# The first weight chunk of a two-layer decoder trunk: ScalarE's table by a copy of a constant, the first weights split ahead of the first features, the first token tile's three products ahead of the second tile's transposes

## The chip, the cores and the metric

One Trainium2 chip, one of its NeuronCores. The metric is the device time of one execution in microseconds (us); lower is better. The time before is a median of 3 executions.

## What is computed

A decoder trunk of two layers over 256 tokens of width 1024, all in float32. Each layer is a half-step SwiGLU feed-forward block, a mixer (a gated linear recurrence with 4 heads beside causal attention with forget gates and 8 heads), cross-attention to 256 memory tokens, and a second half-step feed-forward block. Every block has an RMS norm ahead of it and adds to the residual. The change lies in the first block alone, whose core is:

```python
def rms_norm(x, w):
    x32 = x.astype(jnp.float32)
    y = x32 * lax.rsqrt(jnp.mean(x32 * x32, axis=-1, keepdims=True) + EPS)
    return (y * w.astype(jnp.float32)).astype(x.dtype)

def swiglu(h, w_gate, w_up, w_down):
    return (jax.nn.silu(h @ w_gate) * (h @ w_up)) @ w_down

x = x + 0.5 * swiglu(rms_norm(x, ffn1_norm[l]), ffn1_w_gate[l], ffn1_w_up[l], ffn1_w_down[l])
```

## The kernel before, in words

**Products in three parts.** Each float32 matrix product is made of three products of rounded halves. An operand is split into a high part (rounded to the format that TensorE takes at full rate) and a low part (the operand minus its high part); high times high, high times low and low times high are summed in PSUM. So each piece of weights passes ScalarE, which writes `whi` from the raw piece (L149, or L153 where the norm's gain is multiplied in), and then VectorE, which writes `wlo` (L150 or L154). Features pass the same two engines in `put_split` (L368): ScalarE writes `xfh` (L369), VectorE `xfl` (L370).

**Weights.** `plan` lists all weight pieces in order of use; `fetch` starts their transfers on SyncE's queue into a pool of three `raw` buffers, 1 MB each. The first two pieces are fetched in four quarters of 128 x 512 each, and the input `x` (tile `xs`, in four blocks: token tile t, half j of the width) goes between them: block (0, 0), first quarter, block (1, 0), the other three quarters, blocks (0, 1) and (1, 1).

**The first chunk** (`first_chunk`, L482) makes the first 512 columns of `x @ w_gate` for both token tiles of 128, each into its own PSUM bank (`psa_[0]`, `psa_[1]`). The norm is not applied to the features here: its gain is multiplied into the weights and its scale applied afterwards, so the features are `x` itself, transposed. `turn(t, b)` transposes four 128 x 128 blocks of token tile t on TensorE into the PSUM tile `pt` (L495); `put` splits them; `split_block(i, k)` splits quarter k of weight piece i; `part(kt, t, which)` is one product of 128 x 128 features by 128 x 512 weights (L505), where `which` is 0 for high by high, 1 for high features by low weights (`wlo`), 2 for low features (`xfl`) by high weights. `block(kt)` is the six products of one quarter for both token tiles.

**What sets the order.** Inside `with in_order()` (L201) every engine's instructions are chained in the order in which the code is written, so that each engine takes them one by one as written and waits with all behind it when an operand is missing. The chunk is written as: transposes of the first token tile, six dummy transposes of the identity matrix into an unused bank (`warm_up`, L225), the split of these features, the split of the first weight quarter, two products of the first token tile, the transposes of the second token tile, their split, and then the rest. Ahead of it (L231 to L235) stand nine more dummy transposes and the transpose of the norm's gain (`g0t`, copied to `g0`, by which L153 and L154 multiply).

**ScalarE's table.** The building tools put an `ACT_TABLE_LOAD` ahead of the first ScalarE operation that needs one, here the split of the first features (L369).

Of the kernel before, what the change touches and what calls it, by code (L numbers as in the profile page):

```python
# [8 lines left out]
F32 = mybir.dt.float32  # L9
# [8 lines left out]
P = 128  # L18
# [27 lines left out]
def hymba_kernel(  # L46
# [6 lines left out]
    nc = tc.nc  # L53

    cp = ctx.enter_context(tc.tile_pool(name="cp", bufs=1))
# [10 lines left out]
    def nm(s):  # L66
        uid[0] += 1
        return f"{s}_{uid[0]}"

    def s4(shape, dt=F32, name="s4"):  # L70
        return sp.tile(shape, dt, name=nm(name), tag="s4")

    def small(cols, name="sc", rows=P, bufs=0):
        return sm.tile([rows, cols], F32, name=nm(name), tag=name, bufs=bufs or 4)

    def acc(name="acc"):
        return psa.tile([P, 512], F32, name=nm(name), tag="acc")

    def smp(name="smp"):
        return pss.tile([P, 512], F32, name=nm(name), tag="smp")  # L80
# [48 lines left out]
    def fetch(i):  # L129
        while len(raws) <= min(i, len(plan) - 1):  # L130
            src, nk, cw, _ = plan[len(raws)]
            r = rawp.tile([P, 4 * 520], F32, name=nm("raw"), tag="raw")
            rv = r[:, :nk * cw].rearrange("p (k c) -> p k c", k=nk)
            n = 4 if len(raws) < 2 else 1
            for k0 in range(0, nk, nk // n):
                nc.sync.dma_start(out=rv[:, k0:k0 + nk // n, :], in_=src[:, k0:k0 + nk // n, :])
                for t, j in ({0: [(1, 0)], 3: [(0, 1), (1, 1)]}.get(k0, []) if not raws else []):
                    load_x(t, j)
            raws.append(r)
# [5 lines left out]
    def split_k(i, sl, k, hi, lo):  # L145

        gk = plan[i][3]
        if gk is None:
            nc.scalar.copy(out=hi, in_=sl)  # L149
            nc.vector.tensor_tensor(out=lo, in0=sl, in1=hi.bitcast(F32), op=ALU.subtract)  # L150
        else:
            g = gcols[gk[0]][:, gk[1] + k:gk[1] + k + 1]
            nc.scalar.mul(hi, sl, g)  # L153
            nc.vector.scalar_tensor_tensor(out=lo, in0=sl, scalar=g, in1=hi.bitcast(F32), op0=ALU.mult,  # L154
                                           op1=ALU.subtract)

    def split_block(i, k):

        if k == 0:
            fetch(i + LA_D - 1)  # L160
            pieces.append([])
        cw = plan[i][2]
        if k % 2 == 0:
            slot[:] = [wp.tile([P, SLOT], F32R, name=nm(n), tag=n) for n in ("whi", "wlo")]
        sl = slice(k % 2 * cw, (k % 2 + 1) * cw)
        hi, lo = slot[0][:, sl], slot[1][:, sl]
        split_k(i, raws[i][:, k * cw:(k + 1) * cw], k, hi, lo)
        pieces[i].append((hi, lo))
        return [(hi, lo)]
# [30 lines left out]
    @contextmanager  # L200
    def in_order():  # L201

        traced = nc.cur_bb.bb.instructions
        n = len(traced)
        yield
        prev = {}
        for i in traced[n:]:
            if i.engine in prev:
                tc.add_manual_dep(i, prev[i.engine], mybir.DependencyInfo(mybir.DependencyClass.NoSync,
                                  mybir.DependencyReason.DATA), reason="in_order")  # L210
            prev[i.engine] = i.name
# [6 lines left out]
        fetch(i)  # L218


    ident = cp.tile([P, P], F32, name="ident")
    make_identity(nc, ident)
    warm = acc("warm")

    def warm_up(n):  # L225
        for i in range(n):
            nc.tensor.transpose(warm[:, (i % 4) * P:(i % 4 + 1) * P], ident, ident)
# [3 lines left out]
    with in_order():  # L231
# [1 line left out]
        nc.tensor.transpose(g0t[:, 0:8], grow, ident[0:8, 0:8])  # L233
        nc.vector.tensor_copy(out=g0, in_=g0t[:, 0:8])
        gcols["first"] = g0  # L235
    neghalf = cp.tile([P, 4], F32, name="neghalf")
    nc.vector.memset(neghalf, -0.5)

    lbr = cp.tile([24, P], F32, name="lbr")

# [100 lines left out]
    def inv_rms(ss, rs):  # L341
        ms = small(1, "ms")
        nc.vector.scalar_tensor_tensor(out=ms, in0=ss[:, 0:1], scalar=EPS, in1=ss[:, 1:2], op0=ALU.add, op1=ALU.add)
        nc.gpsimd.tensor_tensor(out=rs, in0=ms, in1=neghalf[:, 0:1], op=ALU.pow)  # L344

    def half(ap, j):
        return ap[:, j * 512:(j + 1) * 512]
# [20 lines left out]
    def put_split(hi, lo, src):  # L368
        nc.scalar.copy(out=hi, in_=src)  # L369
        nc.vector.tensor_tensor(out=lo, in0=src, in1=hi.bitcast(F32), op=ALU.subtract)  # L370
# [79 lines left out]
    def xstat(f, cw, ps):  # L450
        ps += [acc() for _ in range(NT)]
        for kb in range(2):
            pc = take()
            for j in range(4):
                c = 0.0
                for t in range(NT):
                    c += xmm(ps, f, 4 * kb + j, t, pc[j], cw)
                yield c
# [23 lines left out]
    def first_chunk(f, psa_, psb_):  # L482


        psa_ += [acc(), acc()]
        rs = [small(1, "rs0", bufs=2) for _ in range(NT)]
        sq = [s4([P, D], F32, "sq") for _ in range(NT)]
        sums = [small(2, "ss") for _ in range(NT)]
        pa = []

        def turn(t, b):
            pt = smp("pt")
            for j in range(4):
                kt = 4 * b + j
                nc.tensor.transpose(pt[:, j * P:(j + 1) * P], xs[:, t, kt * P:(kt + 1) * P], ident)  # L495
            return pt

        def put(pt, t, b):
            sl = slice(t * P, (t + 1) * P)
            put_split(f.h[b][:, :, sl], f.l[b][:, :, sl], pt.rearrange("p (k t) -> p k t", k=4))  # L500

        def part(kt, t, which):
            x = (f.hi, f.hi, f.lo)[which](kt, t)
            w = (pa[kt][0], pa[kt][1], pa[kt][0])[which]
            nc.tensor.matmul(psa_[t], lhsT=x, rhs=w, start=kt == 0 and which == 0, stop=kt == KT - 1 and which == 1)  # L505

        def block(kt, order=(0, 2, 1)):
            first = order[:2] if order[1] == 2 else order[:1]
            for t in range(NT):
                for w in first:  # L510
                    part(kt, t, w)
            for w in order[len(first):]:
                for t in range(NT):
                    part(kt, t, w)

        def squares(t):
            x = xs[:, t, :]
            nc.scalar.activation(sq[t][:, 0:512], half(x, 0), AF.Square, scale=1.0 / 32.0, accum_out=sums[t][:, 0:1])
            nc.vector.tensor_tensor_reduce(out=sq[t][:, 512:1024], in0=half(x, 1), in1=half(x, 1), scale=1.0 / 1024.0,
                                           scalar=0.0, op0=ALU.mult, op1=ALU.add, accum_out=sums[t][:, 1:2])  # L520

        with in_order():
            p0 = turn(0, 0)
            warm_up(6)
            put(p0, 0, 0)
            pa += split_block(0, 0)
            part(0, 0, 0)
            part(0, 0, 2)
            p1 = turn(1, 0)
            put(p1, 1, 0)  # L530
            part(0, 0, 1)
            for w in (0, 2, 1):
                part(0, 1, w)
            for kt in (1, 2):
                pa += split_block(0, kt)
                block(kt)
            pa += split_block(0, 3)
            p = [turn(t, 1) for t in range(NT)]
            block(3)
            pa += split_block(1, 0)  # L540
            for t in range(NT):
                put(p[t], t, 1)
            block(4, (0, 1, 2))
            for kt in (5, 6, 7):
                pa += split_block(1, kt - 4)
                if kt < 7:
                    squares(kt - 5)
                block(kt)
            taken[0] = 2
            for t in range(NT):  # L550
                inv_rms(sums[t], rs[t])
        yield 16 * T512
        yield from xstat(f, 512, psb_)
        rb = sq[0].rearrange("p (j t) -> p j t", j=8)
        pt = smp("rt")
        for t in range(NT):
            nc.vector.tensor_scalar(out=rb[:, t, :], in0=ident, scalar1=0.0, scalar2=rs[t], op0=ALU.mult, op1=ALU.add)
            nc.tensor.transpose(pt[:, t * P:(t + 1) * P], rb[:, t, :], ident)
        row = sm.tile([P, S], F32, name=nm("L"), tag="L", bufs=1)
        nc.vector.tensor_copy(out=row, in_=pt[:, 0:S])  # L560
        hrs = [small(1, "hrs0", bufs=2) for _ in range(NT)]
        for t in range(NT):
            nc.vector.tensor_scalar(out=hrs[t], in0=rs[t], scalar1=0.5, scalar2=None, op0=ALU.mult)
        return rs, hrs, row
# [652 lines left out]
```

## Time and profile before

| What | Value |
|---|---|
| median of 3 executions | 1234.5 us (1234.41 to 1234.55) |
| the profiled execution's own time | 1234.01 us |
| its span in the profile | 1232.1 us |
| TensorE matmuls busy | 1220.0 us (99% of the span) |
| TensorE weight loads busy | 1116.9 us (91%) |
| VectorE busy | 769.5 us (62%) |
| ScalarE busy | 650.9 us (53%) |
| GpSimd busy | 37.5 us (3%) |
| moved by DMA | 218.67 MB, mean 177 GB/s |

How to read it: the span runs from the first to the last instruction of one profiled execution, and that execution's own time is 1.9 us longer than its span. PE is TensorE's matmuls, PEld its weight loads, which overlap the matmuls; DVE is VectorE, ACT ScalarE, POOL GpSimd, SP SyncE, whose queue (SPq) issues the transfers. A row of a timeline has its start, its length, the engine, the line, the operation, and out<-in with the shape; "x4" means four in a row, whose length is that of all four; in brackets stands how long the engine had been idle and what released it. L505 is line 505 of the kernel. Matmuls are pipelined: the next starts before the one ahead has ended, so their pace is read from start to start, or from the chain of waits, which counts only what each adds.

### The profile page before, as it was taken

How to read it: one execution, taken by the hardware profiler on the slowest of the kernel's cores; microseconds unless marked ns; L12 is line 12 of the kernel's file. 1: busy time of each engine (PE TensorE's matmuls, PEld its weight loads, DVE VectorE, ACT ScalarE, POOL GpSimd, SP SyncE). 2: the span in 40 equal slices, each digit the busy share in tenths (PEclk: the TensorE clock that was granted, in tenths of full speed). 3: DMA queues.
4: the chain of work that ended last, by engine and by line, in shares of the span. 5: the costliest groups of instructions: out<-in, count | busy, mean ns of one | idle time of the engine just before them, and what ended most of it. 6: DMA issues, size and time to landing. Idle time of an engine off the chain costs nothing.

```text
span 1232.1 us, 21551 instructions
## 1 busy us (share of the span) xinstructions
PE 1220.0 (99%) x9037; PEld 1116.9 (91%) x9037; DVE 769.5 (62%) x1186; ACT 650.9 (53%) x1014; POOL 37.5 (3%) x50
## 2 busy tenths in 40 slices
PE   9999999999999999999999999999999999999997
PEld 7999888999889889998889998889998898999986
DVE  6866647588866665454474464476787766545643
ACT  7655435578754454444354354266686555443532
POOL 0000000011000000000000000000110000000000
PEclk9999999999999999999999999999999999999999
DMA  8655655643544374565474556465434533555640
GB/s 300 201 181 174 243 186 169 218 149 103 182 156 159 108 251 165 178 208 204 135 256 138 205 197 213 137 220 167 147 138 171 189 135 122 195 180 171 240 171 35
DMA packets 100001, 218.67 MB, mean 177 GB/s; under 512 B 4128, under 2 KB 16704, under 8 KB 99904
## 3 DMA queue, kind: packets, MB, share of 16 engines
q1 hardware_dynamic: 99744, 217.03, 51.8%
q8 instruction: 71, 1.16, 0.4%
q10 hardware_dynamic: 160, 0.27, 0.1%
q14 instruction: 26, 0.21, 0.0%
HBM read 216.23 MB, written 1.05 MB: 176 GB/s over the span
## 4 chain that ended last, share of the span: by engine, by line
PE 92%; DVE 4%; issue 2%; ACT 1%; POOL 1%; DMA 0%; POOLq 0%; ACTq 0%
PE acc L442 28%; PE acc L443 28%; PE acc L444 28%; DVE wlo L150 1%; PE acc L505 1%; PE al L771 1%; DVE wlo L154 1%; PE pt L363 1%; POOL rs L344 1%; DVE xfl L370 0%; POOL hrs L840 0%; PE cpo L443 0%; ACT pp L895 0%; PE cs L444 0%; PE cs L443 0%
## 5 line engine op out<-in xcount | busy, mean ns | idle before, releaser
L150 DVE TENSOR_TENSOR wlo<-raw,whi 128x1024 fp32r<-128x1024 f32 (+1 forms) x324 | 388.8, 1223 | 265.0 <-ACT whi L149 264.2
L149 ACT CAST whi<-raw 128x1024 fp32r<-128x1024 f32 (+1 forms) x324 | 330.2, 1048 | 276.3 <-PE acc L444 137.1
L442 PE MATMUL acc<-xfh,whi 128*128 128x256 f32 x1536 | 432.2, 282 | 0.0
L443 PE MATMUL acc<-xfl,whi 128*128 128x256 f32 x1536 | 430.7, 280 | 0.3 <-DVE xfl L370 0.2
L444 PE MATMUL acc<-xfh,wlo 128*128 128x256 f32 x1536 | 429.8, 280 | 0.0
L443 PEld LDWEIGHTS acc<-xfl,whi 128*128 128x128 f32 x1536 | 289.3, 188 | 0.9 <-DVE xfl L370 0.7
L444 PEld LDWEIGHTS acc<-xfh,wlo 128*128 128x128 f32 x1536 | 289.4, 188 | 0.0
L442 PEld LDWEIGHTS acc<-xfh,whi 128*128 128x128 f32 x1536 | 288.5, 188 | 0.8
L443 PE MATMUL acc<-wlo,hth 128*128 128x512 f32 (+1 forms) x352 | 136.2, 387 | 0.0
L442 PE MATMUL acc<-whi,hth 128*128 128x512 f32 (+1 forms) x352 | 136.0, 386 | 0.0
L444 PE MATMUL acc<-whi,htl 128*128 128x512 f32 (+1 forms) x352 | 135.6, 385 | 0.0
L442 PE MATMUL acc<-whi,xfh 128*128 128x512 f32 (+1 forms) x240 | 88.0, 367 | 0.0
L443 PE MATMUL acc<-wlo,xfh 128*128 128x512 f32 (+1 forms) x240 | 87.4, 364 | 0.0
L444 PE MATMUL acc<-whi,xfl 128*128 128x512 f32 (+1 forms) x240 | 87.1, 363 | 0.0
L442 PEld LDWEIGHTS acc<-whi,hth 128*128 128x128 f32 x352 | 66.1, 188 | 14.3 <-DVE sil L738 0.2
L444 PEld LDWEIGHTS acc<-whi,htl 128*128 128x128 f32 x352 | 66.2, 188 | 14.2
L443 PEld LDWEIGHTS acc<-wlo,hth 128*128 128x128 f32 x352 | 66.1, 188 | 13.8
L154 DVE SCALAR_TENSOR_TENSOR wlo<-raw,g,whi 128x512 fp32r<-128x512 f32 (+1 forms) x96 | 62.0, 702 | 19.2 <-PE acc L444 11.4
L153 ACT ACTIVATE whi<-raw,g 128x512 fp32r<-128x512 f32 (+1 forms) x96 | 58.4, 677 | 17.7 <-PE acc L443 14.9
L369 ACT CAST hth<-sil 128x512 fp32r<-128x512 f32 x36 | 22.3, 619 | 57.7 <-DVE sil L738 57.7
L444 PEld LDWEIGHTS acc<-whi,xfl 128*128 128x128 f32 x240 | 45.1, 188 | 7.6
L442 PEld LDWEIGHTS acc<-whi,xfh 128*128 128x128 f32 x240 | 45.1, 188 | 7.7
(274 smaller groups left out, 1547.4 us busy)
## 6 DMA issues: line engine op xcount, KB each, us to landing
raw<-in_ffn_w_down_dram SPq DMA_DIRECT2D x44, 1024.0 KB, 4.8
raw<-in_ffn_w_up_dram SPq DMA_DIRECT2D x40, 1024.0 KB, 5.3
raw<-in_ffn_w_gate_dram SPq DMA_DIRECT2D x38, 1024.0 KB, 5.2
raw<-in_w_in_dram SPq DMA_DIRECT2D x24, 1024.0 KB, 5.3
raw<-in_cross_wk_dram SPq DMA_DIRECT2D x8, 1024.0 KB, 5.4
raw<-in_cross_wv_dram SPq DMA_DIRECT2D x8, 1024.0 KB, 5.0
raw<-in_w_out_dram SPq DMA_DIRECT2D x8, 1024.0 KB, 4.8
raw<-in_cross_wq_dram SPq DMA_DIRECT2D x8, 1024.0 KB, 5.1
```

What stands on the lines that cost most here:

```text
L149: nc.scalar.copy(out=hi, in_=sl)
L150: nc.vector.tensor_tensor(out=lo, in0=sl, in1=hi.bitcast(F32), op=ALU.subtract)
L153: nc.scalar.mul(hi, sl, g)
L154: nc.vector.scalar_tensor_tensor(out=lo, in0=sl, scalar=g, in1=hi.bitcast(F32), op0=ALU.mult, op1=ALU.subtract)
L344: nc.gpsimd.tensor_tensor(out=rs, in0=ms, in1=neghalf[:, 0:1], op=ALU.pow)
L363: nc.tensor.transpose(pt[:, j * P:(j + 1) * P], hn[:, kt * P:(kt + 1) * P], ident)
L369: nc.scalar.copy(out=hi, in_=src)
L442: nc.tensor.matmul(ps, lhsT=lh, rhs=rh, start=start, stop=False)
L443: nc.tensor.matmul(ps, lhsT=lh, rhs=rl, start=False, stop=False)
L444: nc.tensor.matmul(ps, lhsT=ll, rhs=rh, start=False, stop=stop)
L505: nc.tensor.matmul(psa_[t], lhsT=x, rhs=w, start=kt == 0 and which == 0, stop=kt == KT - 1 and which == 1)
L771: nc.tensor.matmul(ps[s0:s0 + hb, c0:c0 + hb], lhsT=k[:, h, a:a + hb], rhs=rhs[:, h, a + step:a + step + hb], start=True, stop=True)
```

## The change

Two edits. The first moves the constant tile `neghalf` (4 columns of -0.5) up to the head of the program and adds a ScalarE copy of one of its columns into a new tile `first_act`, as ScalarE's first operation. The second rewrites the head of the first chunk: the first weight quarter is split ahead of the first features; the dummy transposes are four instead of six and come after that split in the code; the first token tile's products are taken in the order high-high, low weights, low features, and all three stand ahead of the second token tile's transposes; the second tile's three products take the same order.

```diff
+    neghalf = cp.tile([P, 4], F32, name="neghalf")
+    nc.vector.memset(neghalf, -0.5)
+
+    nc.scalar.copy(out=cp.tile([P, 1], F32, name="first_act"), in_=neghalf[:, 0:1])
     ident = cp.tile([P, P], F32, name="ident")
     make_identity(nc, ident)
     warm = acc("warm")
...
-    neghalf = cp.tile([P, 4], F32, name="neghalf")
-    nc.vector.memset(neghalf, -0.5)
...
         with in_order():
             p0 = turn(0, 0)
-            warm_up(6)
+            pa += split_block(0, 0)
             put(p0, 0, 0)
-            pa += split_block(0, 0)
-            part(0, 0, 0)
-            part(0, 0, 2)
+            warm_up(4)
+            for w in (0, 1, 2):
+                part(0, 0, w)
             p1 = turn(1, 0)
             put(p1, 1, 0)
-            part(0, 0, 1)
-            for w in (0, 2, 1):
+            for w in (0, 1, 2):
                 part(0, 1, w)
             for kt in (1, 2):
                 pa += split_block(0, kt)
```

TensorE's order at the head of the chunk, before. `pt_134` and `pt_155` are the transposed features of the first and second token tile, `acc_126` and `acc_127` their PSUM banks; `warm_101` takes the dummies.

```order
L495 MATMUL pt_134<-ident,xs 128x128 x4
L227 MATMUL warm_101<-ident 128x128 x6
L505 MATMUL acc_126<-whi_149,xfh_122 128x512
L505 MATMUL acc_126<-whi_149,xfl_123 128x512
L495 MATMUL pt_155<-ident,xs 128x128 x4
L505 MATMUL acc_126<-wlo_150,xfh_122 128x512
L505 MATMUL acc_127<-whi_149,xfh_122 128x512
L505 MATMUL acc_127<-whi_149,xfl_123 128x512
L505 MATMUL acc_127<-wlo_150,xfh_122 128x512
```

And now, where the two tiles are `pt_136` and `pt_156`, the banks `acc_128` and `acc_129`, and all lines from here on stand two lower:

```order
L497 MATMUL pt_136<-ident,xs 128x128 x4
L231 MATMUL warm_105<-ident 128x128 x4
L507 MATMUL acc_128<-whi_143,xfh_124 128x512
L507 MATMUL acc_128<-wlo_144,xfh_124 128x512
L507 MATMUL acc_128<-whi_143,xfl_125 128x512
L497 MATMUL pt_156<-ident,xs 128x128 x4
L507 MATMUL acc_129<-whi_143,xfh_124 128x512
L507 MATMUL acc_129<-wlo_144,xfh_124 128x512
L507 MATMUL acc_129<-whi_143,xfl_125 128x512
```

The product with `wlo` of the first token tile has moved ahead of the second tile's transposes, and in both tiles the product with `xfl` has become the last of the three.

ScalarE's order at its start, before. `raw_83` is the first weight piece.

```order
L369 ACT_TABLE_LOAD
L369 CAST xfh_122<-pt_134 128x4x128
L153 ACTIVATE whi_149<-raw_83,g_102 128x512
L369 CAST xfh_122<-pt_155 128x4x128
L153 ACTIVATE whi_149<-raw_83,g_102 128x512
```

And now:

```order
L224 ACT_TABLE_LOAD
L224 COPY first_act<-neghalf 128x1
L153 ACTIVATE whi_143<-raw_83,g_106 128x512
L371 CAST xfh_124<-pt_136 128x4x128
L371 CAST xfh_124<-pt_156 128x4x128
L153 ACTIVATE whi_143<-raw_83,g_106 128x512
```

One copy is new, and the first `whi` stands ahead of the first `xfh`. VectorE has the matching swap of its first `wlo` and `xfl`. Apart from names and line numbers, the rest of these three orders, and all of SyncE's and GpSimd's, is as before. The new tile lies in the pool of constants ahead of everything that is allocated later: in the built program the first `raw` buffer starts at byte 30304 of each partition instead of 30272, and the buffers of the split weights and features have moved up by the same 32 bytes; before, they started at multiples of 64 bytes. `xs` has not moved.

## Prediction

> **What bounds the kernel now.** I read the page's busy shares and chain first, then the chain of waits in its first 20 us, then the timelines of the stretch that the change rewrites.
>
> ```profile
> PE 1220.0 (99%) x9037; PEld 1116.9 (91%) x9037; DVE 769.5 (62%) x1186; ACT 650.9 (53%) x1014; POOL 37.5 (3%) x50
> PE 92%; DVE 4%; issue 2%; ACT 1%; POOL 1%; DMA 0%; POOLq 0%; ACTq 0%
> ```
>
> TensorE is busy for 99% of the span and makes up 92% of the chain. So the whole kernel is one stream of products; a change can only shorten it where TensorE stands still, and 12 us of idle time are all there is. The chain's start (time, length, what):
>
> ```profile
> 0.74 3.16 DMA xs<-in_x_dram
> ...
> 3.94 1.11 PE pt L495 x4
> 5.05 1.28 PE warm L227 x6
> ...
> 9.25 3.50 PE acc L505 x14
> 12.75 0.87 PE pt L495 x8
> 13.63 6.99 PE acc L505 x30
> ```
>
> After 9.25 the stream is dense: 30 products in 6.99 are 0.233 each. Before it, it is full of holes. Six dummy transposes take 1.28, 0.213 each, while eight real ones of the same size at 12.75 take 0.87, 0.109 each: TensorE's clock doubles in between. The holes, first on ScalarE, then on VectorE, then on TensorE:
>
> ```profile
> 1.38 1.28 ACT L369 ACT_TABLE_LOAD   x1 [1.38 <-PEq L1204]
> 5.09 0.59 ACT L369 CAST xfh<-pt 128x512 fp32r<-128x512 f32 x1 [2.43 <-PE pt L495]
> 5.57 0.72 ACT L153 ACTIVATE whi<-raw,g 128x512 fp32r<-128x512 f32 x1
> 7.89 0.59 ACT L369 CAST xfh<-pt 128x512 fp32r<-128x512 f32 x1 [1.59 <-PE pt L495]
> 8.37 1.34 ACT L153 ACTIVATE whi<-raw,g 128x512 fp32r<-128x512 f32 x2
> ```
> ```profile
> 3.78 0.17 DVE L234 COPY g<-g0t 128x8 f32<-128x8 f32 x1 [2.33 <-PE g0t L233]
> 5.71 0.69 DVE L370 TENSOR_TENSOR xfl<-pt,xfh 128x512 fp32r<-128x512 f32 x1 [1.76 <-ACT xfh L369]
> 6.33 0.75 DVE L154 SCALAR_TENSOR_TENSOR wlo<-raw,g,whi 128x512 fp32r<-128x512 f32 x1
> 8.51 0.69 DVE L370 TENSOR_TENSOR xfl<-pt,xfh 128x512 fp32r<-128x512 f32 x1 [1.43 <-ACT xfh L369]
> 9.13 1.41 DVE L154 SCALAR_TENSOR_TENSOR wlo<-raw,g,whi 128x512 fp32r<-128x512 f32 x2
> ```
> ```profile
> 6.35 0.80 PE L505 MATMUL acc<-whi,xfh 128*128 128x512 f32 x1
> 6.94 0.47 PE L505 MATMUL acc<-whi,xfl 128*128 128x512 f32 x1
> 7.25 0.60 PE L495 MATMUL pt<-ident,xs 128*128 128x128 f32 x4
> 7.61 0.48 PE L505 MATMUL acc<-wlo,xfh 128*128 128x512 f32 x1
> 8.53 0.50 PE L505 MATMUL acc<-whi,xfh 128*128 128x512 f32 x1 [0.44 <-ACT xfh L369]
> 9.25 0.50 PE L505 MATMUL acc<-whi,xfl 128*128 128x512 f32 x1 [0.23 <-DVE xfl L370]
> 9.59 0.39 PE L505 MATMUL acc<-wlo,xfh 128*128 128x512 f32 x1
> 9.82 0.39 PE L505 MATMUL acc<-whi,xfh 128*128 128x512 f32 x1
> ```
>
> The reader is to see one path across the three: the second token tile's transposes (7.25), ScalarE's `xfh` (7.89), VectorE's `xfl` (8.51), the product that takes it (9.25). While TensorE waits for this `xfl` it has one product (8.53) to do. The `wlo` product, whose weights are ready long before, stands behind the wait at 9.59, and only at 9.82 does the next quarter begin.
>
> **The table copy.** The table load stands at 1.38 already, behind no wait; ScalarE then sits idle until 5.09. The change keeps the load there and adds one copy of 128 x 1 behind it. The trace has no such copy; the shortest row above is 0.59 for 512 columns, so I put it between 0 and 0.59, in a stretch of 2.43 idle us. It waits for a constant that VectorE writes first in its queue, as before. I take 0. The cover is the idle time up to 4.6, where the first `whi` can start (below); a copy that ended later than that would push all behind it.
>
> **The swap on ScalarE and VectorE.** The first `whi` now stands ahead of the first `xfh` and waits for the gain (3.78 + 0.17 = 3.95) and for the first weight quarter, whose issue and landing one answer gives:
>
> ```profile
> L136 SPq DMA_DIRECT2D raw<-in_ffn_w_gate_dram x1: 417/417/417, 1.2 to 1.2; - x1
> ...
> DMA to landing us min/median/max: 3.4/3.4/3.4
> ```
>
> Issued at 1.2, it lands at 4.6. So `whi` runs from 4.6 to 5.3 (0.72). Two `whi` in a row take 1.34, so the next operation starts 1.34 - 0.72 = 0.62 after the first; `xfh`, whose transposes are done at 5.05, runs from 5.2 to 5.8, 0.1 later than before. On VectorE `wlo` follows the end of `whi` by 0.04, as at 6.33: 5.35 to 6.1. The pace there is 1.41 - 0.75 = 0.66, so `xfl` runs from 6.0 to 6.7, 0.3 later than before. Behind the first `xfh` ScalarE waits for the second tile's transposes, as before, and the second quarter's `whi` waits with it.
>
> **The first token tile on TensorE.** Two dummies less save 2 x 0.213: it is free at 5.05 + 4 x 0.213 = 5.90 instead of 6.33. The high-high product waits for `xfh` at 5.8 and starts at 5.9 instead of 6.35, so the dummies dropped were cover, not work. Before, the second product began 0.59 behind the first; now the `wlo` product (weights ready at 6.1) begins at 6.5. At the slow clock a product takes twice 0.233, less the part that runs ahead: I take 0.43, which puts the `xfl` product (ready at 6.75) at 6.9. The transposes came 0.31 behind the last product and do so again: 7.2 instead of 7.25. Three products now stand ahead of them instead of two, and yet they are 0.05 earlier, since the first began 0.45 earlier and the third costs about 0.4. The second tile's features are there by then: their transfer
>
> ```profile
> L143 SPq DMA_DIRECT2D xs<-in_x_dram x1: 424/424/424, 1.6 to 1.6; - x1
> ...
> DMA to landing us min/median/max: 5.1/5.1/5.1
> ```
>
> was issued at 1.6 and landed at 6.7.
>
> **The second token tile.** From the transposes on, the path is as before and 0.05 earlier: the high-high product at 8.48, the `xfl` product at 9.20. In the 0.72 between them the `wlo` product now runs too; it is one product of 0.233. Behind the `xfl` product comes the next quarter at once: 9.20 + (9.59 - 9.25) = 9.54, where it was 9.82. **Sum: 0.23 + 0.05 = 0.28 us.**
>
> **What keeps or eats it later.** The second quarter's `whi` ends at 8.37 + 0.72 - 0.05 = 9.04, half a microsecond ahead of 9.54. TensorE's order after that is unchanged, so its stream moves as one. ScalarE and VectorE stop gaining where ScalarE meets a transfer: the second `up` piece is issued at 12.3, lands 7.5 later, at 19.8, and its split has no earlier start to gain.
>
> ```profile
> L136 SPq DMA_DIRECT2D raw<-in_ffn_w_up_dram x1: 379/379/379, 12.3 to 12.3; - x1
> ...
> DMA to landing us min/median/max: 7.5/7.5/7.5
> ```
> ```profile
> 20.45 0.39 PE L442 MATMUL acc<-whi,xfh 128*128 128x512 f32 x1
> ```
>
> But TensorE only begins the `up` chunk at 20.45, with the first `up` piece, whose 24 products at 0.233 last until 26; the wait costs it nothing. So 0.28 stays to the end: the profiled execution goes from 1234.01 (span 1232.1 and 1.9 around it) to 1233.7. It lay 0.5 below the median of the runs, which I carry along: 1234.5 - 0.28 = **1234.2 us**, 0.02%. A measurement of this kernel can tell about 0.2%, 2.5 us, from no change; this is a ninth of that.
>
> **Rivals.**
>
> *The wait is filled but nothing is won (1234.5).* The third product ahead of the transposes is the weak term. The first product took 0.59 to the next one's start, not 0.43; if the third does too, and the transposes slip by a tenth more, the second tile's path starts 0.2 late and eats the 0.23 of the filled wait. Bounds: 1234.35 to 1234.55.
>
> *The clock rises later (slower, 1235.1).* The doubling falls near 7: the product at 6.35 still took 0.59 to the next, and the four transposes from 7.25 took 0.60 in all, where four at 3.94 took 1.11. What went ahead of it was 3 us, from 3.94 on, of nothing but transposes, and the change takes two dummies out of these. If as much again were needed, the work from 7.2 to 10 would run at half pace: four transposes on the path (4 x 0.105 = 0.4), part of the two products ahead of `xfl` (0.2), and the `xfl` product with what follows until 10 (0.3). That is 0.9, so 0.6 slower than before. It decides from about 1 us of delay on. Against it: TensorE's gap ahead of the first product is no longer than before (5.90 to 5.9), and its products start 0.45 earlier.
> The Trainium skill, TensorE: Matmul & The Clock Gate, Part 1, has full clock granted after a busy window of some 3.4 us that runs free of the kernel; by that a lost window would be 3.4 us instead of my 3, and the time 1235.2 instead of 1234.2. The trace, with its doubling behind 3 us of near-gapless transposes, fits that. Part 4 of that page has transposes not counted as busy in the same way; this trace speaks against it, since little else had run.
>
> *The first weight quarter lands later (slower, 1235.0).* Before, ScalarE came to it at 5.57, a microsecond behind its landing; now both of ScalarE's first operations wait for it at 4.6. If it landed 1 us later, `xfl` would be ready at 7.75 and the transposes would come at 8.0 instead of 7.25: 0.75 late, less 0.23 for the filled wait, 0.5 slower. It decides from about 0.4 us of delay on. Against it: the order of transfers is unchanged, and the three runs lie within 0.14 us.
>
> *The addresses (slower, 1240, or the other way).* All weight and split feature buffers start 32 bytes higher, off a multiple of 64. If that slowed the stream of 1220 us by half a per cent, it would cost 6 us, and from 0.2% on it outweighs all else. The nearest rows speak against it:
>
> ```profile
> L443 PE MATMUL acc<-xfl,whi 128*128 128x256 f32 x1536 | 430.7, 280 | 0.3 <-DVE xfl L370 0.2
> ...
> L443 PE MATMUL acc<-wlo,xfh 128*128 128x260 f32 x64 | 18.1, 282 | 0.0
> ```
>
> The 260-column pieces lie 1040 bytes apart, so three of four start 16, 32 or 48 bytes off, and their products take 282 ns against 280 for 256 columns. Weight loads from such addresses are not in these rows.
>
> **How the numbers follow.** Forecast 0.69, its own range 1234.0 to 1234.4 (0.1 for the landing, 0.1 for the third product). Nothing won 0.12, clock 0.08, late weights 0.06, addresses 0.05 (0.04 slower, 0.01 faster). The range takes in the first four cases, and at its low end a part of the 0.5 by which one execution already lay below the median: 1233.7 to 1235.1. Only the addresses pass 0.2%: faster 0.01, same 0.95, slower 0.04.
>
> **What would show it.** Right: table load still at 1.4; first `whi` at 4.6, ahead of `xfh` at 5.2; first product at 5.9; second tile's transposes at 7.2; the product with its `xfl` at 9.2, with two products ahead of it in the wait; the next quarter at 9.5; from there TensorE's rows 0.28 earlier up to the end. Wrong: transposes of the second tile past 7.4, or 0.2 us apiece there (clock), a first `whi` past 5 (landing), a longer mean than 280 ns for the products of 256 columns (addresses).

## The result, and the profile after

The changed kernel takes 1238.55 us in the median of 12 executions (1236.75 to 1240.74); the kernel before, run beside it, 1234.55 (12 executions). The ratio is 1.0027 (95% interval 1.002 to 1.0035): slower by at least 0.2%, and above the forecast range of 1233.7 to 1235.1. The 12 times of the changed kernel fall into two groups of six, 1236.75 to 1237.70 and 1239.40 to 1240.74, about 2.3 us apart. The profiled execution is of the upper group: 1239.46, span 1237.4, which is 5.3 longer than the span of before. The page's busy shares, and the engines' shares of the chain:

```profile
PE 1225.3 (99%) x9035; PEld 1120.7 (91%) x9035; DVE 769.4 (62%) x1186; ACT 650.8 (53%) x1015; POOL 37.2 (3%) x50
PE 94%; DVE 3%; ACT 1%; POOL 1%; issue 1%; DMA 0%; POOLq 0%; ACTq 0%
```

VectorE and ScalarE are as busy as before to 0.1 us. TensorE is busy 5.3 us longer, with two dummies fewer to do. So the loss is no wait: the same products take longer.

The head of the chunk in the chain (time, length, what):

```profile
5.09 0.85 PE warm L231 x4
...
5.97 1.71 PE acc L507 x3
7.69 0.87 PE pt L497 x4
...
9.21 5.63 PE acc L507 x15
14.84 0.87 PE pt L497 x8
15.72 6.51 PE acc L507 x28
```

Before, the eight transposes at the end of the stage began at 12.75; now at 14.84, 2.09 later. The four transposes at 7.69 take 0.87, 0.217 each, where the eight at 14.84 take 0.109 each: at 7.69 the clock has not doubled yet. The timelines of ScalarE, VectorE and TensorE:

```profile
1.36 1.28 ACT L224 ACT_TABLE_LOAD   x1 [1.36 <-PEq L1205]
2.65 0.19 ACT L224 COPY first_act<-neghalf 128x1 f32<-128x1 f32 x1
4.73 0.72 ACT L153 ACTIVATE whi<-raw,g 128x512 fp32r<-128x512 f32 x1 [1.89 <-DMA raw<-in_ffn_w_gate_dram]
5.36 0.56 ACT L371 CAST xfh<-pt 128x512 fp32r<-128x512 f32 x1
```
```profile
5.48 0.75 DVE L154 SCALAR_TENSOR_TENSOR wlo<-raw,g,whi 128x512 fp32r<-128x512 f32 x1 [1.54 <-ACT whi L153]
6.15 0.68 DVE L372 TENSOR_TENSOR xfl<-pt,xfh 128x512 fp32r<-128x512 f32 x1
```
```profile
5.97 0.79 PE L507 MATMUL acc<-whi,xfh 128*128 128x512 f32 x1
6.57 0.63 PE L507 MATMUL acc<-wlo,xfh 128*128 128x512 f32 x1
6.99 0.69 PE L507 MATMUL acc<-whi,xfl 128*128 128x512 f32 x1
7.49 1.05 PE L497 MATMUL pt<-ident,xs 128*128 128x128 f32 x4
9.21 0.79 PE L507 MATMUL acc<-whi,xfh 128*128 128x512 f32 x1 [0.68 <-ACT xfh L371]
...
12.37 1.05 PE L507 MATMUL acc<-wlo,xfh 128*128 128x512 f32 x2
13.22 0.47 PE L507 MATMUL acc<-whi,xfh 128*128 128x512 f32 x1
13.52 0.40 PE L507 MATMUL acc<-whi,xfl 128*128 128x512 f32 x1
```

ScalarE and VectorE do what was forecast, 0.2 late at most. On TensorE, products follow each other by 0.42 at first (6.57 to 6.99), the two from 12.37 to 13.22 still do, and from 13.22 on it is 0.30, then 0.23 by the chain's pieces (28 in 6.51): the clock doubles near 13.3 instead of near 7. Each trace also keeps the times at which the granted clock changed: full clock is granted from 7.11 on before, from 13.36 on after. Where a time is given below from which a run has full clock, it is from this record.

That is 2.1 of the 5.3 us. The rest comes later, bit by bit. A landmark is the 48 transposes of `fpt`, whose row gives the first and the last start; the first row is of before, the second of after:

```profile
L951 PE MATMUL fpt<-ident,pp x48: 270/272/328, 302.6 to 936.9; 128*128 128x128 f32 x48
```
```profile
L952 PE MATMUL fpt<-ident,pp x48: 270/273/329, 305.4 to 941.4; 128*128 128x128 f32 x48
```

After is 2.1 late at 13, 2.8 late at 302, 4.5 late at 937 and 5.3 late at the end of the span. No new wait stands between. From the start of one matmul to the next, some 5780 gaps of the trace are between 100 and 130 ns, nine in ten of them between products of 256 columns; their mean is 117.29 ns before and 117.64 after, 0.3% more. For products of 512 columns (some 2060 gaps of 200 to 260 ns) it is 231.04 before and 231.59 after. That is 2.0 us from the narrow products and 1.1 from the wide ones. The groups, whose lengths are modelled, show little of it:

```profile
L445 PE MATMUL acc<-xfl,whi 128*128 128x256 f32 x1536 | 431.4, 281 | 0.4 <-DVE xfl L372 0.4
L446 PE MATMUL acc<-xfh,wlo 128*128 128x256 f32 x1536 | 430.4, 280 | 0.0
```

So there are two questions: why the stream runs 0.3% slower (**the drift**, 3 us), and why the clock rises 6 us later (**the late rise**, 2 us, in the profiled execution; no execution of the lower group was profiled).

### The profile page after: what moved, and what is told of

It is laid out like the page before. It is cut to its first block, busy times and chain, and to the rows that moved or that the text cites. A ratio compares the mean times of both kernels' runs of the same rounds, so it can differ in the third digit from the quotient of the medians.

```text
span 1237.4 us, 21548 instructions
## 1 busy us (share of the span) xinstructions
PE 1225.3 (99%) x9035; PEld 1120.7 (91%) x9035; DVE 769.4 (62%) x1186; ACT 650.8 (53%) x1015; POOL 37.2 (3%) x50
## 4 chain that ended last, share of the span: by engine, by line
PE 94%; DVE 3%; ACT 1%; POOL 1%; issue 1%; DMA 0%; POOLq 0%; ACTq 0%
PE acc L444 29%; PE acc L445 29%; PE acc L446 29%; PE acc L507 1%; DVE wlo L150 1%; PE al L772 1%; PE pt L365 1%; DVE wlo L154 1%; POOL hrs L841 0%; PE cpo L445 0%; ACT pp L896 0%; PE cs L445 0%; PE cs L446 0%; PE cs L444 0%; PE fpt L952 0%
```

## The experiments

In each set the kernel before ran on the same chip; "before" below is its median there.

### The addresses, and the dummies

My theory at this point was the rival on record: the 32 bytes by which the large buffers moved cause the drift, and the two dummies dropped cause the late rise. Against it stood that something else of the change causes either. Four kernels, before at 1234.29.

`e1_addr_only`, the kernel before with a new constant of 32 bytes that nothing uses:

```diff
+    cp.tile([P, 8], F32, name="pad")
     ident = cp.tile([P, P], F32, name="ident")
```

> The kernel before with one more constant tile of 32 bytes ahead of the identity matrix and no other edit, so that all weight and feature buffers lie 32 bytes higher, as in the changed kernel. Address theory (the steady drift of 3 us between the two traces, products of 256 columns 117.6 ns apart instead of 117.3, comes from the addresses): the doubling of the clock stays near 7 us, the start is as before, the drift appears, time 1237.5. Rival (the drift is a state of the chip that comes and goes from run to run, whatever the addresses): most runs at 1234.5, a few 3 higher, no different from the kernel before.

Measured: 1234.20 (11 executions), ratio 1.0002 (0.9993 to 1.001). TensorE is busy 1219.9 us, as before, and the gaps of the trace are 117.30 ns in the mean. The 32 bytes cost nothing that can be told.

`e2_old_addr`, the changed kernel whose copy goes into a fifth column of `neghalf`, so that the large buffers lie at their old addresses:

```diff
-    neghalf = cp.tile([P, 4], F32, name="neghalf")
+    neg5 = cp.tile([P, 5], F32, name="neghalf")
+    neghalf = neg5[:, 0:4]
     nc.vector.memset(neghalf, -0.5)
-    nc.scalar.copy(out=cp.tile([P, 1], F32, name="first_act"), in_=neghalf[:, 0:1])
+    nc.scalar.copy(out=neg5[:, 4:5], in_=neghalf[:, 0:1])
```

> The changed kernel with the ScalarE copy going into a fifth column of the constant's own tile, so that the buffers lie where they lay before the change. Address theory: the clock still doubles near 13 us, which costs 2.1, but the drift is gone: 1236.6 in every run. Rival (state of the chip): runs in two groups, near 1237 and 1239.5, as with the changed kernel.

Measured: 1237.57 (7 executions: four at 1236.84 to 1237.57, three at 1238.91 to 1239.53), ratio 1.0029 (1.0018 to 1.0039). The drift is still there: the gaps of its trace are 117.63 ns in the mean. My theory of the addresses fell, from both sides.

The late rise is not in this trace, although the profiled execution, 1238.91, is of the upper group: it has full clock from 7.95 on. What delays it stands in the second layer. The waits between 870 and 930 us (us in all, times, longest), first of the changed kernel, then of `e2_old_addr`:

```profile
ACT whi L153 <- DMA raw<-in_cross_wk_dram: 4.9, 1, 4.9
```
```profile
ACT whi L153 <- DMA raw<-in_cross_wk_dram: 6.9, 1, 6.9
PE al L773 <- DVE kk L796: 0.6, 1, 0.6
PE ax L817 <- DVE kk L796: 0.5, 1, 0.5
```

ScalarE waits 2 us longer for a transfer of cross-attention weights. On VectorE the tile `kk` of the recurrence stands behind the `wlo` of these weights, and TensorE waits 1.1 us for it. Six of the 18 traces have this **late transfer** (a wait of 6.0 to 7.2 on ScalarE, and 0.5 to 1.4 of TensorE for `kk`): `e1_addr_only`, `e2_old_addr`, `e4_after_6_dummies`, `f3_after_wlo_back`, `g1_after_wlo_back` and `g3_wlo_back_5_dummies`. In the other twelve ScalarE waits 4.8 to 5.2, and TensorE not at all. Every engine's order in `e1_addr_only` is that of the kernel before, so the order is not its cause; most likely it comes and goes with the execution. Why is open. So an execution that takes 2 us more need not be one with a late clock.

`e3_before_4_dummies`, the kernel before with `warm_up(4)` in place of `warm_up(6)`:

> The kernel before with four dummy transposes instead of six and nothing else. Dummy theory (the two dummies less are what delays the clock): TensorE idles from 5.9 to 6.35, the clock doubles near 13 instead of 7, and the time is 2 to 2.5 higher, 1236.6 to 1237. Rival (the delay comes from something else in the new order, such as the products that now stand ahead of the transposes): doubling at 7, 1234.5.

Measured: 1236.40 (11 executions: five at 1233.77 to 1235.14, six at 1236.40 to 1237.08), ratio 1.0009 (1.0 to 1.0018). The profiled execution, 1237.08, is of the upper group. TensorE there, in the timeline:

```profile
4.74 1.06 PE L227 MATMUL warm<-ident 128*128 128x128 f32 x4
6.24 0.79 PE L505 MATMUL acc<-whi,xfh 128*128 128x512 f32 x1 [0.44 <-ACT whi L153]
...
12.44 1.05 PE L505 MATMUL acc<-wlo,xfh 128*128 128x512 f32 x2
13.30 0.43 PE L505 MATMUL acc<-whi,xfh 128*128 128x512 f32 x1
13.56 0.40 PE L505 MATMUL acc<-whi,xfl 128*128 128x512 f32 x1
```

TensorE stands still for 0.44 where the two dummies were, and full clock comes at 13.36. `fpt` runs from 305.4 to 939.7, 634.3 us apart as before, and the gaps are 117.30 ns: a late rise without drift. It makes the trace 2.1 late at 31 us; another 0.7, up to `fpt`, is a wait in the first layer's mixer.

`e4_after_6_dummies`, the changed kernel with `warm_up(6)`:

> The changed kernel with six dummy transposes instead of four. They end at 6.35, so the first product starts 0.4 later than in the changed kernel. Dummy theory: the clock doubles near 7 again and the start is about as before; what is left is the drift, 1234.3 without it and up to 1237.5 with it. Rival (not the dummies): doubling still near 13, 1237 to 1239.7.

Measured: 1237.22 (9 executions, two of them at 1238.55 and 1238.75), ratio 1.0022 (1.0012 to 1.0031). Drift without a late rise: in the profile full clock comes at 6.06, TensorE is still busy 1223.3 us, and the gaps are 117.64 ns. The profiled execution, 1238.75, has the late transfer too, for which TensorE waits 1.4 us; without it, it would stand at 1237.35, among the other seven.

This pair also shows what the new order is worth. In the profiles of `e1_addr_only` (order of before) and `e4_after_6_dummies` (new order) the clock doubles at about the same time, near 6:

```profile
6.43 0.50 PE L506 MATMUL acc<-whi,xfh 128*128 128x512 f32 x1 [0.22 <-ACT whi L153]
6.76 0.40 PE L506 MATMUL acc<-whi,xfl 128*128 128x512 f32 x1
7.00 0.60 PE L496 MATMUL pt<-ident,xs 128*128 128x128 f32 x4
...
8.99 0.50 PE L506 MATMUL acc<-whi,xfl 128*128 128x512 f32 x1 [0.22 <-DVE xfl L371]
...
9.56 0.39 PE L506 MATMUL acc<-whi,xfh 128*128 128x512 f32 x1
```
```profile
5.99 0.51 PE L507 MATMUL acc<-whi,xfh 128*128 128x512 f32 x1
6.34 0.39 PE L507 MATMUL acc<-wlo,xfh 128*128 128x512 f32 x1
6.76 0.50 PE L507 MATMUL acc<-whi,xfl 128*128 128x512 f32 x1
7.10 0.60 PE L497 MATMUL pt<-ident,xs 128*128 128x128 f32 x4
...
9.10 0.51 PE L507 MATMUL acc<-whi,xfl 128*128 128x512 f32 x1
9.44 0.39 PE L507 MATMUL acc<-whi,xfh 128*128 128x512 f32 x1
```

The new order has the transposes 0.10 later, because the third product waits for `xfl`, and the next quarter (9.44) 0.12 earlier. In `e1_addr_only` the first features landed later (its first transposes begin at 4.02, those of `e4_after_6_dummies` at 3.94); with equal landings, I estimate, as little as 0.04 is left. In before's own profile the next quarter came at 9.82: the time at which the clock doubles moves it more than the order does.

### The placement, first try

What else differed between `e4_after_6_dummies` and before? The instructions are the same but for the head. The places of the buffers are not. `whi` and `wlo` take seven buffers each in turn, of 4160 bytes, in one pool, and the building tools give out the places in the order in which buffers are asked for and come free in their plan. Numbering the 14 places in the built programs, `whi` goes through 0, 6, 5, 4, 1, 2, 3 in both kernels. `wlo` goes through 7, 13, 12, 11, 8, 9, 10 before, each seven behind its `whi`, and through 7, 13, 12, 8, 9, 10, 11 after: four of seven have moved. No listing of the order shows it, since names there carry no places.

Theory now: the drift comes from these four places. Rival: from the new order at the head. Each kernel of this set gives every buffer a place by hand (`wt`), HI and LO being the sequences of places of `whi` and of `wlo` (LO counted from 7):

```diff
+    HI, LO = (0, 6, 5, 4, 1, 2, 3), (0, 6, 5, 4, 1, 2, 3)
+    at = {"whi": 0, "wlo": 0}
...
+    def wt(n):
+        j = (HI if n == "whi" else LO)[at[n] % N_W]
+        at[n] += 1
+        return wp.tile([P, SLOT], F32R, name=nm(n), tag=f"{n}{j}", bufs=1)
...
-                hi = wp.tile([P, SLOT], F32R, name=nm("whi"), tag="whi")
-                lo = wp.tile([P, SLOT], F32R, name=nm("wlo"), tag="wlo")
+                hi = wt("whi")
+                lo = wt("wlo")
```

`f1_before_placed` is the kernel before with these LO; `f2_before_wlo_moved` has LO = (0, 6, 5, 1, 2, 3, 4), the places of after; `f3_after_wlo_back` is the changed kernel with the places of before; `f4_wlo_back_9_dummies` is that with `warm_up(6)`, and `warm_up(3)` behind the second tile's split.

> The kernel before with the seven wlo buffers and the seven whi buffers placed by hand, each buffer where the pool had put it. The control for the next run: 1234.3 with products 117.3 ns apart, a few runs 2 higher when the clock rises late.

> The same kernel, but with the wlo buffers in the order in which they lie in the changed kernel (four of the seven in another place); no instruction differs from the control. Placement theory (the drift of 3 us over the whole kernel comes from where the wlo buffers lie, which the changed order of the code moved): products 117.6 ns apart, 1237.4. Rival (the drift comes from the new order or from the copy): as the control, 1234.3.

> The changed kernel with the wlo buffers placed as they lay before the change. Placement theory: products 117.3 ns apart, the drift gone; what is left is the start, 1234.0 where the clock rises early and 1236.3 where it rises late, about half of the runs each as with the other kernels of four dummies. Rival (order or copy): two groups at 1237.2 and 1239.4 as the changed kernel.

> The changed kernel with the wlo buffers placed as before the change, six dummies again, and three more behind the second token tile's transposes, in TensorE's wait for its xfh. If a window of TensorE's activity that starts at random sets the clock, the extra dummies fill the last hole and late rises become rare: 1234.0 in nearly all runs, a little below the kernel before. If the late rise has another cause, a fifth to a half of the runs are still 2 higher.

Measured (5 executions each, before at 1234.28): `f1_before_placed` 1240.72 (ratio 1.0048, 1.0035 to 1.0061), `f2_before_wlo_moved` 1242.84 (1.0066, 1.0052 to 1.008), `f3_after_wlo_back` 1239.75 (1.0043, 1.003 to 1.0055), `f4_wlo_back_9_dummies` 1240.08 (1.0049, 1.0036 to 1.0061). All four are 5 us slow or more, for a reason of my making: placed by hand, the scheduler put four `whi` of the next weight piece ahead of the features of the second half of the width on ScalarE. TensorE in the profile of `f1_before_placed`, and its clock there:

```profile
18.37 1.27 PE L515 MATMUL acc<-whi,xfh 128*128 128x512 f32 x2 [3.21 <-ACT xfh L379]
```
```profile
17.80:21.20 3.40, 2.83 (x7) 0.50 0.54 134
21.20:24.60 3.40, 3.40 (x10) 0.50 0.76 260
24.60:28.00 3.40, 3.40 (x16) 1.00 0.95 325
```

In the second fence the columns are stretch, length, TensorE busy, clock, DMA share and GB/s. A wait of 3.2 us cost the clock as well: half until 24.6. So only the four among themselves can be compared. `fpt` runs 309.1 to 943.3 in `f1_before_placed` (634.2 apart), 309.1 to 945.1 in `f2_before_wlo_moved` (636.0), and the gaps are 117.31 and 117.64 ns: the drift follows the places of `wlo`. But times under such a disturbance settle nothing.

### The placement, alone

The same with one line more in the first chunk, `split(3)` at the end of its ordered part, which leaves every engine's order as it was. Before at 1234.13.

`g1_after_wlo_back`, the changed kernel with the LO of before:

> The changed kernel, every engine's order unchanged, with the wlo buffers placed where they lay before the change. Placement theory: products 117.3 ns apart; two groups of runs, 1234.0 (clock rises early, the change's start 0.3 ahead) and 1236.2 (late), about half each. Rival (the drift belongs to the new order): 1237.2 and 1239.4.

Measured: 1234.17 (11 executions), ratio 1.0001 (0.9992 to 1.001). All of the change is in it, and the drift is gone. `g2_before_wlo_moved`, the kernel before with the LO of after:

> The kernel before, every engine's order unchanged, with four of the seven wlo buffers moved to where they lie in the changed kernel. Placement theory: products 117.6 ns apart, 1237.4, with a run in seven or so 2 higher. Rival: 1234.3.

Measured: 1237.13 (8 executions), ratio 1.0028 (1.0018 to 1.0038). Nothing of the change is in it but the four places, and the drift is there. In the built programs the `wlo` buffers are the only ones that lie elsewhere, in `g2_before_wlo_moved` than before and in `g1_after_wlo_back` than in the changed kernel. The busy times, first of `g1_after_wlo_back`, then of `g2_before_wlo_moved`:

```profile
PE 1222.1 (99%) x9035; PEld 1118.2 (91%) x9035; DVE 769.5 (62%) x1186; ACT 650.5 (53%) x1015; POOL 37.0 (3%) x50
```
```profile
PE 1222.4 (99%) x9037; PEld 1118.7 (91%) x9037; DVE 769.4 (62%) x1186; ACT 650.8 (53%) x1014; POOL 36.9 (3%) x50
```

The two busy times look alike and are not. The profiled execution of `g1_after_wlo_back` is its slowest, 1237.2, with full clock from 12.93 on: the 2.1 above before's 1220.0 are the late rise, and the gaps are 117.28 ns. (Its span is 3.2 longer than before's, since it has the late transfer too.) In `g2_before_wlo_moved` full clock came at 5.35, before the first product, and the 2.4 are drift: 117.63 ns. The wide products agree: 231.06 and 231.60 ns.

`g3_wlo_back_5_dummies` is `g1_after_wlo_back` with `warm_up(5)`. `g4_wlo_back_no_holes` leaves no hole among the dummies: ten ahead of the gain's transpose instead of nine, five in the chunk, and three in the wait behind the second tile's transposes.

```diff
-        warm_up(9)
+        warm_up(10)
...
-            warm_up(4)
+            warm_up(5)
...
             put(p1, 1, 0)
+            warm_up(3)
```

> As the first of these runs, with five dummy transposes, which end just when the first product can start, so that TensorE doesn't idle there. Window theory (a window of TensorE's activity, starting at random, must be nearly full): late rises fall from a half to a fifth or less, median 1234.0. If the number of dummies itself were what counts, late rises would still be as frequent as with four.

> As the run with five dummies, with a tenth dummy ahead of the gain's transpose and three in the wait behind the second token tile's transposes, so that hardly any hole is left up to the first dense stretch. Window theory: no late rise at all or one that comes a window earlier, 1234.0 in every run, 0.3 below the kernel before's fast runs. Rival: the dummies in the wait delay the second tile's products by 0.2 and nothing is gained, 1234.3.

Measured: `g3_wlo_back_5_dummies` 1234.20 (11 executions, two at 1236.44 and 1236.88), ratio 1.0002 (0.9993 to 1.0011). `g4_wlo_back_no_holes` 1233.85 (11 executions, 1233.55 to 1234.33), ratio 0.9996 (0.9987 to 1.0005): the median can't be told from before's, but there is no upper group, and the profiled one has full clock from 5.38 on. TensorE in the timeline of the latter:

```profile
4.84 0.98 PE L241 MATMUL warm<-ident 128*128 128x128 f32 x5
5.91 0.49 PE L517 MATMUL acc<-whi,xfh 128*128 128x512 f32 x1
...
7.16 0.60 PE L507 MATMUL pt<-ident,xs 128*128 128x128 f32 x4
7.60 0.49 PE L241 MATMUL warm<-ident 128*128 128x128 f32 x3
8.43 0.50 PE L517 MATMUL acc<-whi,xfh 128*128 128x512 f32 x1 [0.35 <-ACT xfh L381]
```

### Which property of the places

Theory: `wlo` has to lie a fixed seven places from its `whi`. Rival: `wlo`'s own places or their sequence count. All on `g4_wlo_back_no_holes`, before at 1233.83; the edit is the line of HI and LO, here for `h1_both_rings_moved`, then `h2_only_whi_moved`, then `h3_ascending`. `h4_pairs` has the third line too, but its places are laid out with `whi` and `wlo` in turn, a piece's two side by side.

```diff
-    HI, LO = (0, 6, 5, 4, 1, 2, 3), (0, 6, 5, 4, 1, 2, 3)
+    HI, LO = (0, 6, 5, 1, 2, 3, 4), (0, 6, 5, 1, 2, 3, 4)
+    HI, LO = (0, 6, 5, 1, 2, 3, 4), (0, 6, 5, 4, 1, 2, 3)
+    HI, LO = (0, 1, 2, 3, 4, 5, 6), (0, 1, 2, 3, 4, 5, 6)
```

> The changed kernel without holes among its dummies (1233.85 us with the old placement), all orders the same; whi and wlo both lie in the rotated sequence 0, 6, 5, 1, 2, 3, 4, so that each wlo is again seven buffers behind its whi. Theory of the distance: no drift, 1233.9 us, 117.3 ns per 256-column product. Rival (wlo's own places): wlo no longer lies as in the kernel before, so about 1237 us and 117.6 ns.

> As h1, but wlo lies as in the kernel before and only whi is rotated, so that the distance between whi and wlo of a piece is no longer the same for all seven. Theory of the distance: about 1237 us, 117.6 ns. Rival (wlo's own places): no drift, 1233.9 us and 117.3 ns.

> As h1, with both rings in ascending order, 0 to 6 and 7 to 13, distance seven throughout. Theory of the distance: 1233.9 us, 117.3 ns. Rival: wlo's sequence is a new one, so anything from 1232 to 1237 us.

> As h1, with whi at the even places and wlo at the odd ones, so that a piece's two buffers lie side by side, at a distance of one buffer throughout. If only an equal distance counts: 1233.9 us. If the distance of seven itself counts, or wlo's places: 1237 us or another pace.

Measured (10 executions each): `h1_both_rings_moved` 1233.68 (ratio 0.9998, 0.9988 to 1.0007), `h2_only_whi_moved` 1233.66 (0.9996, 0.9987 to 1.0006), `h3_ascending` 1234.06 (0.9997, 0.9988 to 1.0006), `h4_pairs` 1235.44 (1.0009, 0.9999 to 1.0018; all ten between 1235.18 and 1236.28). As accounts of the kernel's time both theories fall. `h1_both_rings_moved` has `wlo` exactly where the changed kernel has it, and no loss, against the rival; `h2_only_whi_moved` breaks the distance of four pairs, and shows no loss either, against the theory. It is the combination of the two rings that costs 3 us in the changed kernel, and 1.6 in the pairs.

But the time of `h2_only_whi_moved` hides two shifts. Mean gaps from start to start, in ns; the nine traces with the places of before differ by 0.07 at most, the five with those of the changed kernel by 0.05:

| Places | 256 columns | 512 columns |
|---|---|---|
| of before (nine traces) | 117.27 to 117.33 | 231.00 to 231.07 |
| of the changed kernel (five) | 117.63 to 117.64 | 231.59 to 231.64 |
| `h1_both_rings_moved` | 117.25 | 230.96 |
| `h2_only_whi_moved` | 117.48 | 230.28 |
| `h3_ascending` | 117.18 | 231.35 |
| `h4_pairs` | 117.33 | 231.69 |

In `h2_only_whi_moved` the narrow products lose 1.2 us and the wide ones win 1.5. In nearly all narrow ones the weights are the operand that is loaded into TensorE (`lhsT` at L574 of the kernel before), in the wide ones they are the one that streams through it (`rhs` at L447 and L647). So for the narrow products the theory of the distance still fits all six rows: they are slow where four pairs have a distance of their own, and at the old pace wherever one distance holds throughout. That is a fit, not a test. The wide products follow another rule, and by what mechanism either is set stays open.

## Why the prediction was wrong

**The step that failed.** "TensorE's order after that is unchanged, so its stream moves as one." The order was unchanged, the pace was not: 117.64 ns for a product of 256 columns instead of 117.29 and 231.59 for one of 512 instead of 231.04, because the order in which the code asks for buffers had put four of the seven `wlo` buffers elsewhere. This is shown from both sides (`g1_after_wlo_back`, `g2_before_wlo_moved`). It is 3 of the 4 us between the medians.

**A second step that failed.** "... so the dummies dropped were cover, not work." They were no product's work, but the clock counted them. With four dummies full clock came at 12.93 to 13.67 in four of the five traces, one of them of the kernel before (`e3_before_4_dummies`), with six at 5.35 to 7.71 in all seven. How many of the executions without a trace rose late is not known: six of 12 of the changed kernel and six of 11 of `e3_before_4_dummies` are in the upper group, but `e2_old_addr` shows that such a one can have another cause. The evidence in the prediction, that TensorE's gap ahead of its first product is no longer than before, was true and did not help: what counts is not this one gap.

**The rival of the clock** was right in its mechanism and too small in its size: 0.9 above the forecast by the text, 2.4 measured (2.1 above before and the 0.28 not won). I let the doubling slip by one stretch of 3 us, from 7.2 to 10; it slipped to 13.36, 6.26 later, and every product until then ran at half pace.

**The rival of the addresses** looked at the right thing, where the buffers of the weights lie, and at the wrong property of it. The 32 bytes cost nothing (`e1_addr_only`, `e2_old_addr`), as its evidence of the 260-column products said: those with `wlo` took 282 ns before and after. The places within the pool were not looked at. The sign that I named for it, a mean above 280 ns, was there: 281 in one group of three.

**The steps of the head** were right while the clock was. The table load stayed at 1.4, and the copy took 0.19 in idle time. The first weights did not land later in any way that mattered: `whi` began at 4.73 after and at 4.60 in `e4_after_6_dummies`, forecast 4.6. There the transposes came at 7.10, the `xfl` product at 9.10, the next quarter at 9.44, each 0.1 earlier than forecast. But the gain was counted against before's profile, in which the clock doubled near 7. Against an execution of the old order with the same clock it is 0.12, not 0.28: the `xfl` product comes 0.11 later than in the old order (9.10 and 8.99), as in the rival in which nothing is won, and takes back half of the 0.23. And of the 0.12, about 0.08 is the earlier landing of the first features. With the places put back, no difference can be told from none: 1234.17 and 1234.13.

**The sum.** 3 us of drift in every execution, less about 0.1, on before's 1234.55 give 1237.4, and with 2.1 to 2.4 of late rise 1239.7; the two groups lie at 1236.75 to 1237.70 and 1239.40 to 1240.74. The profiled execution of the upper group, 1239.46, is such a one, without the late transfer; that its five neighbours are too is likely, not shown.

## What to carry to other kernels

When TensorE is busy for 99% of the span, compare the places of the buffers in the two built programs and not only the order of the instructions: a change of a few lines in one stage can reassign a pool that the whole kernel uses, and 0.3% on each product outweighs all that the stage can win. Take the pace of each kind of product by itself: a total can hide a loss in one and a gain in another. Before a wait or a filler at the start of TensorE's work is called free, ask how much of it keeps the clock up; fill the holes with dummies (as `g4_wlo_back_no_holes` does, 1233.85 and never above 1234.33) rather than cut them. And read a gain of tenths of a us against an execution with the same clock, and read the cause of a late end from the trace, not from the time.

## What the runs showed of the hardware

- **The clock has a window of its own.** In the profile of `f1_before_placed` it fell at 17.8 and rose at 24.6; by the record it was full for 10.24 us before and half for 6.83, three and two stretches of 3.41. The kernel before doubled its clock near 7.1 in one execution, and with the same head near 5.9 (`e1_addr_only`). The Trainium skill, TensorE: Matmul & The Clock Gate, Part 1, has a window of 3.4 us that runs free of the kernel; these numbers agree. What they add is how much two dummies of 0.213 us weigh. `g1_after_wlo_back` and `e4_after_6_dummies` have the same order but for them, and their rises, at 12.93 and 6.06, lie 6.87 apart, two windows: so their windows ended at nearly the same times, and with six dummies the one that ended at 6.1 was enough, with four neither it nor the next. In the traces full clock came at 13.36, 7.95, 13.36, 12.93 and 13.67 with four dummies (the changed kernel, `e2_old_addr`, `e3_before_4_dummies`, `g1_after_wlo_back`, `f3_after_wlo_back`), at 7.76 with five, at 5.35 to 7.71 in the seven with six, and at 4.52 to 6.07 in `g4_wlo_back_no_holes` and the four built on it. By time alone, 18 of 41 executions lie more than 1.9 us above the fastest of their kernel in the first four of these kernels, 20 of 137 in those with six dummies (the kernel before, `e1_addr_only`, `e4_after_6_dummies`, `g2_before_wlo_moved`), and none of 51 in the last five; these counts hold delays of every cause, the late transfer among them. How busy a window must be to count was not measured.
- **Transposes raise the clock.** In `g4_wlo_back_no_holes` the five dummies at 4.84 take 0.98, less than the four in `e3_before_4_dummies` (1.06), and the next product starts 0.33 behind the first (0.59 before). Only transposes had run. In `h2_only_whi_moved` full clock came at 4.52, also behind nothing but transposes. Part 4 of that page of the Trainium skill has them not counting as busy in the same way; the traces speak against it.
- **The place of a weight buffer sets the pace of products.** 117.3 or 117.6 ns per 256 columns, 231.1 or 231.6 per 512, 1234.1 or 1237.1 us, by four places of seven. The Trainium skill, SBUF — State Buffer, SBUF: two separate sides, says that TensorE, ScalarE and VectorE's own ports never wait on anyone. By that rule the places should not matter through the other engines; `g2_before_wlo_moved` shows that they matter. Whether the engines meet at the memory after all or TensorE's own reads meet each other, no run here tells.
